# Loading and splitting the down weights at other stages in the last block of a hybrid decoder step

## The chip, the cores and the metric

The kernel runs on one core of one Trainium2 chip. The metric is device time in microseconds (us) of one execution, as a median over runs; it is compared with the kernel before on the same chip.

## The reference, cut to what matters

One decoder layer is computed in float32 for 2048 prompt positions and 32 sample rows (8 sequences of 4): attention and a gating unit, an output projection, and then a SwiGLU feed-forward network with 1024 model columns and 2816 hidden columns.

```python
def _swiglu(x, g, w_gate, w_up, w_down):
    h = _rmsnorm(x, g)
    return (jax.nn.silu(h @ w_gate) * (h @ w_up)) @ w_down
...
    x = x + jnp.concatenate([att, u * gate], axis=-1) @ w_out
    x = x + _swiglu(x, norm2_g, w_gate, w_up, w_down)
```

Only the last line, and in it the product with `w_down`, is concerned here, and that only for the last third of the positions.

## The kernel before

**Blocks and units.** The layer's second half runs over three blocks of tiles of 128 positions: six, six and four. The last block (`B.last`) holds four tiles and the 32 sample rows, whose two halves make five row groups for the down product. In each block the feed-forward network runs over 22 units `f`, one for each 128 hidden columns. A unit has seven stages `q` = 0 to 6, one for each of the seven products of a fast 2x2 matrix multiplication (`product`, L1596). Every float32 operand is held as a high part in a rounded format and a low part (the rest), and a product is made of three matmuls (high x high L1606, high x low L1607, low x high L1608) for each of four slices: 12 matmuls a stage, in the last block with 272 columns each.

**Operands of the products.** Stage `q` of unit `f` also prepares stage `q` of unit `f + 1` (`prepare`, L1570). In the last block ScalarE (ACT) makes the high part (`high`, L1543, its copy stands at L1545), GpSimd (POOL) makes the low part one stage later (`low_half`, L1547, its subtraction at L1549), and SyncE (SP) issues the load of the same source for unit `f + 2` (`load_source`, L1502, its DMA at L1504). Sources `fr` have eight buffers, so that load waits until POOL has made the low part of the source one stage before. Operand pairs `op` have eight buffers too; a high part is written into the buffer of a product that has just ended. In stages 1 and 3 SP also issues a piece of 512 KB of the sample cache's copy, from DRAM to DRAM (`roll`, L1255, DMA at L1258).

**Down weights.** The rows of `w_down` for unit `f`, 128 x 1024, are loaded by SP into `fd` (`load_down`, L1586, DMA at L1588), of which there is one buffer. `split_down` (L1592) splits it by `split_sb` (L132): ACT copies the high part (L135), POOL subtracts for the low part (L138), into a pair `dw`, of which there are two, one for even and one for odd units. `fd` is free for the next load when both have read it. The load of unit `f` is called behind stage 2 of unit `f` (that of unit 0 earlier), its split behind stage 6 where `f` is even, behind stage 5 where it is odd.

**Down product.** The down products of units `f - 2` and `f - 1` run together in the even unit `f`, row groups 0 and 1 behind stage 3, 2 and 3 behind stage 4, the sample rows behind stage 5 (`down_unit`, L1664, matmuls at L1679). A row group of 128 rows has two halves of six matmuls of 512 columns, three on the even unit's `dw` and then three on the odd unit's. The left operands `hw` are written by ACT (L1656, L1660) and DVE (L1274) when a unit ends. DVE adds the sums to the accumulator (L1681). For the last pair of units `last_rows` (L1728) does it, with its first matmuls in `first_downs` (L1683).

**What sets the order.** Each engine, SP's queue too, works through its instructions in the order in which the code calls them; a call that is put at another stage moves every instruction in it on each of these queues. Waits are semaphores that follow from the use of the buffers.

Of the kernel before, what the change touches and what calls it, by code (L numbers as in the profile page):

```python
# [28 lines left out]
NF = FF // P  # L29
# [35 lines left out]
def hymba_step(ctx: ExitStack, tc: tile.TileContext, A: dict, O: dict):  # L65
# [66 lines left out]
    def split_sb(hi, lo, src, eng_hi=None, eng_lo=None):  # L132

        if eng_hi is None:
            act.activation(hi, src, AF.Copy)  # L135
        else:
            eng_hi.tensor_copy(hi, src)
        (eng_lo or pool).tensor_sub(lo, src, hi.bitcast(F32))  # L138
# [540 lines left out]
    for half in range(2):  # L679
        for ki, kind in enumerate(ORDER[half]):  # L680
            for gi, tiles in enumerate(GROUPS):
# [13 lines left out]
                for j, tj in enumerate(tiles):  # L695
# [25 lines left out]
                    else:  # L721
                        layer_norm(e + 1, t, lambda t=t: zn["g", t], P, lambda t=t: gate_tile(t))

                        f = e + 4 + ((3 if half else 5) if tj in (4, 5) else 0)
# [510 lines left out]
    def op_tile():  # L1235

        t_ = pool_["fg"].tile([P, 2, 512], F32R, name="op", tag="op", bufs=8)
        return t_[:, 0], t_[:, 1]
# [6 lines left out]
    def ob_pair(name):  # L1245
        t_ = lo.tile([P, 2, 1024], F32R, name=name, tag="ob", bufs=2)
        return t_[:, 0], t_[:, 1]
# [7 lines left out]
    def roll(n):  # L1255
        for src, dst, b, q in pieces[:n]:
            r0, r1 = q * 256, min((q + 1) * 256, WB - ST)
            sync.dma_start(O[dst][b, r0:r1, :], A[src][b, ST + r0:ST + r1, :])  # L1258
        del pieces[:n]
# [10 lines left out]
    def tick():  # L1270
        clock[0] += 1
        while due and min(due)[0] <= clock[0]:
            fn, args = due.pop(min(due))
            fn(*args)  # L1274
# [35 lines left out]
    def load_wo(half, s, staged):  # L1310
        raws["o", half, s] = w_ = staged()
        r0 = (s + 4) % KD * P
        sync.dma_start(w_, A["w_out"][r0:r0 + P, half * 512:(half + 1) * 512])

    def split_wo(B, half, s, place, eng_lo=None):
        B.wo[half, s] = wh, wl = place(s)
        split_sb(wh, wl, raws.pop(("o", half, s)), eng_lo=eng_lo)
# [252 lines left out]
    def prepare(B, f, s):  # L1570

        if B.b0 == 0:
            for fn, j in (ODD_STAGES if f % 2 else EVEN_STAGES if f else FIRST_STAGES)[s]:
                fn(f, j)
            return
        for fn, j in ((low_half, s - 1), (high, s)):
            if 0 <= j < 7:
                fn(f, j)
        if s < 7 and f + 1 < NF:
            load_source(f + 1, s)  # L1580

    def ahead_of(f, s):
        for fn, j in (ODD_AHEAD if f % 2 else EVEN_AHEAD).get(s, ()):
            fn(f, j)

    def load_down(f):  # L1586
        raws["d", f] = w_ = pool_["fd"]
        sync.dma_start(w_, A["w_down"][f * P:(f + 1) * P, :])  # L1588
# [3 lines left out]
    def split_down(f):  # L1592
        wd[f % FC] = ob_pair("dw")
        split_sb(*wd[f % FC], raws.pop(("d", f)))
# [105 lines left out]
    def final_a(B, i, then=None):  # L1700
        n = B.rows[i]
        y = square_tile()
        if n == SR:
            act.activation(y[0:SR], B.acc[i][SR:2 * SR], AF.Copy)
            dve.tensor_add(B.acc[i][0:SR], B.acc[i][0:SR], y[0:SR])
        s1 = fl.tile([P, 4], F32, name="s1", tag="s1", bufs=6)
        act.activation(y[:n], B.acc[i][:n], AF.Square, accum_out=s1[:n, 0:1])
        later(1, rms_b, s1, n)
        later(2, final_b, B, i, s1, then)
# [92 lines left out]
    B = blocks[0]  # L1802
# [75 lines left out]
    def sources(B, f, *js):  # L1878
        for j in js:
            if B.b0 == 0:  # L1880
                load_quarter(f, j)
            else:
                load_source(f, j)
# [26 lines left out]
    def first_block(B):  # L1910

        m2, m1 = acc_place(2), acc_place(4)
        split_early(B, 1, m1)
        split_early(B, 2, m2)
        B.place()
        load_cat(B, 0, KD - 1, KD)
        load_cat(B, 5, 0, KD)
        merge_load(h, 2)
        load_acc(B, 1)
        load_acc(B, 0)  # L1920
        half1_load(*range(KD))
        sync.dma_start(gain[0], dap(A["final_g"], 0, [[0, P], [1, D]]))
        plan.run(10 ** 9)
        split_early(B, 3)
        for n, what in ((2, [(merge, h, 2, pool), (merge, h, 3, pool), (split_cat, B, 0), (split_early, B, 4)]),
                        (4, [(merge_store, h, 2, 4)]), (5, [(open_end, B, 1)]),
                        (6, [(half1_split, B, 0, 1)]), (7, [(open_end, B, 0), (split_cat, B, 5)]),
                        (8, [(half1_split, B, 2, 3)]), (9, [(half1_split, B, 4, 5), (sources, B, 0, 0, 1, 2, 3)]),
                        (10, [(half1_split, B, 6, 7)]), (11, [(sources, B, 1, 0, 1, 2, 3)])):
            later(n, both, *what)  # L1930
        for i in (1, 2, 3):
            open_unit(B, i)
        open_part(B, 0, (KD - 1,), False, True)
        for i in (4, 5):
            open_unit(B, i)
        first_operands(B)

        p2 = second_unit(B, 2)
        for i in (2, 3):
            load_acc(B, i)  # L1940
        second_end(B, 0, second_unit(B, 0))
        open_end(B, 2)
        second_end(B, 2, p2, 3)
        p1 = second_unit(B, 1)
        for i in (4, 5):
            load_acc(B, i)
        second_end(B, 1, p1)
        p3 = second_unit(B, 3)
        open_end(B, 3)
        second_end(B, 3, p3)  # L1950
        for i in (4, 5):
            open_end(B, i)
        for i in (4, 5):
            second_end(B, i, second_unit(B, i), 1)
# [54 lines left out]
    for bi, B in enumerate(blocks):  # L2009
        if bi == 0:  # L2010
            first_block(B)
        else:
            next_block(B, downs, finals)
        if B.last:
            hs4 = consts.tile([P, 4, 2 * SR], F32R, name="hs4", tag="cats")
        nb = None if B.last else blocks[bi + 1]

        part = 4
        units = [dict(f=f, a=0, b=B.nt) for f in range(NF)]
        if not B.last:  # L2020
            units[0:1] = [dict(f=0, a=0, b=part), dict(f=0, a=part, b=B.nt)]
        rows = list(range(len(B.rows)))
        last_h = {}

        def one(u, q):
            tick()
            product(B, u, q)
            f = u["f"]
            if u["b"] < B.nt:
                if bi == 0 and q in (0, 2):  # L2030
                    sources(B, 2, q, q + 1)
                return

            if f and q < 2:
                prepare(B, f, 7 + q)
            if f + 1 < NF:
                prepare(B, f + 1, q)
            if f + 2 < NF:
                if bi == 0 and f:
                    if q in (0, 2):  # L2040
                        sources(B, f + 2, q, q + 1)
                if bi == 0:
                    ahead_of(f + 2, q)
            elif nb:

                for s in {(0, 2): (0, 1), (0, 4): (2, 3), (1, 3): (4, 5), (1, 5): (6, 7)}.get((f + 2 - NF, q), ()):
                    load_wo(0, s, fraw)
                if f + 1 == NF and q > 0:
                    split_wo(nb, 0, q - 1, lambda s: op_tile())
            if f + 1 < NF and q in (1, 3, 5)[:(1, 3, 2)[bi]]:  # L2050
                roll(1)

            if q == 2 and f:
                load_down(f)
            elif q == (5 if f % 2 else 6):
                split_down(f)

        def downs_of(pair, a, b):
            for i in rows[a:b]:
                down_unit(B, i, pair)  # L2060

        for n, u in enumerate(units):
            u["n"] = n
            for q in range(7):
                one(u, q)
                if u["f"] % 2 == 0 and u["f"] > 0 and 3 <= q < 6:
                    downs_of((B.h[0], B.h[1]), *((0, 2), (2, 4), (4, 9))[q - 3])
        pair = (B.h[0], B.h[1])
        if B.last:
            last_rows(B, pair)  # L2070
        else:

            last = ([4] if nb.last else []) + [i for i in rows if not (nb.last and i == 4)]
            downs = [lambda B=B, pair=pair: first_downs(B, last[0], last[1], pair)]
            downs += [lambda B=B, pair=pair, i=i: down_unit(B, i, pair) for i in last[2:]]
            finals = [lambda B=B, nb=nb, i=i: final_a(B, i, (load_acc, nb, i) if i < len(nb.rows) else None) for i in last]
# [104 lines left out]
```

## Time and profile before

| | us |
|---|---|
| median of 3 runs | 2521.73 |
| lowest and highest | 2508.28 and 2523.93 |
| the profiled execution, its own time | 2527.26 |
| its span | 2525.4 |
| TensorE (PE) busy, share of the span | 97% |
| DVE, ACT, POOL busy | 50%, 45%, 52% |

The profile comes from one execution. In its rows, a group shows line, engine, operation, output and inputs, the number of instructions, busy time and mean duration, and then the idle time just ahead of them with the engine and line that ended it ("<-"). PE is the stream of matmuls, PEld that of weight loads. The last block's 22 units lie between about 2110 and 2500 us.

### The profile page before, as it was taken

Reading aid. Unit: us, or ns where it says so; the run is one execution under the profiler, and the core shown is the slowest. Engines: PE = TensorE matmul, PEld = TensorE weight load, DVE = VectorE, ACT = ScalarE, POOL = GpSimd, SP = SyncE. Lnnn points to the kernel's source line nnn. Section 1 sums busy time; section 2 is a strip of 40 time slices with the busy share of each in tenths; the row PEclk is TensorE's granted clock in tenths of the full one; section 3 lists DMA queues with packets and bytes.
Section 4 is the critical chain, followed back from the end, with each engine's and each line's share of the span. In section 5 each row is a group of like instructions: output and inputs, shape, how many; then the busy total and the mean of one; then the engine's idle time right before and its main releaser. Section 6 shows DMA issues by size and latency. Waiting matters only on the chain.

```text
span 2525.4 us, 39104 instructions
## 1 busy us (share of the span) xinstructions
PE 2442.6 (97%) x14022; PEld 2116.0 (84%) x14022; DVE 1270.2 (50%) x2595; ACT 1130.9 (45%) x2449; POOL 1303.2 (52%) x1019
## 2 busy tenths in 40 slices
PE   8998999999999899999999999999999998999997
PEld 7877776668887678999999989999999978888986
DVE  4558582217776645444444465444444465444444
ACT  7324343226666556454554446233233255333334
POOL 2216441005778447676776626445355445556565
PEclk9999999999999899999999999999999999999999
DMA  9974845675554554555555363535445363555553
GB/s 294 280 230 148 259 127 175 200 253 175 182 168 131 142 191 154 167 175 179 155 194 166 128 218 134 188 136 199 170 169 203 117 223 126 175 200 178 197 174 132
DMA packets 292292, 455.36 MB, mean 180 GB/s; under 512 B 28711, under 2 KB 160984, under 8 KB 286980
## 3 DMA queue, kind: packets, MB, share of 16 engines
q1 hardware_dynamic: 285252, 440.82, 53.6%
q10 hardware_dynamic: 6848, 12.06, 1.7%
q8 instruction: 111, 1.82, 0.3%
q14 instruction: 81, 0.66, 0.1%
HBM read 365.07 MB, written 157.84 MB: 207 GB/s over the span
## 4 chain that ended last, share of the span: by engine, by line
PE 62%; POOL 6%; issue 6%; DVE 3%; DMA 3%; ACT 2%; SPq 0%; POOLq 0%; DVEq 0%; ACTq 0%
PE ps_o L1679 15%; PE ps_m L1608 9%; PE ps_m L1607 9%; PE ps_m L1606 9%; POOL op L1549 4%; PE ps_s L856 3%; PE ps_o L911 2%; PE ps_t L883 1%; PE ps_s L935 1%; PE ps_s L318 1%; PE ps_o L1373 1%; PE ps_o L1375 1%; PE ps_o L1374 1%; PE ps_m L1373 1%; PE ps_m L1375 1%
## 5 line engine op out<-in xcount | busy, mean ns | idle before, releaser
L1549 POOL TENSOR_TENSOR op<-fr,op 128x512 fp32r<-128x512 f32 x385 | 487.5, 1299 | 246.6 <-ACT op L1545 232.5
L1606 PE MATMUL ps_m<-xh,op 128*128 128x384 f32 (+3 forms) x1904 | 604.9, 318 | 0.7 <-DVE zn L1627 0.4
L1608 PE MATMUL ps_m<-xh,op 128*128 128x384 f32 (+3 forms) x1904 | 604.4, 317 | 0.0
L1607 PE MATMUL ps_m<-xl,op 128*128 128x384 f32 (+3 forms) x1904 | 603.9, 317 | 0.1
L1679 PE MATMUL ps_o<-dw,hw 128*128 128x512 f32 x2040 | 492.6, 396 | 20.4 <-POOL dw L138 12.6
L1679 PEld LDWEIGHTS ps_o<-dw,hw 128*128 128x128 f32 x2040 | 385.1, 190 | 106.3 <-POOL dw L138 16.5
L1606 PEld LDWEIGHTS ps_m<-xh,op 128*128 128x128 f32 x1904 | 360.2, 189 | 5.3 <-ACT xh L1450 0.7
L1607 PEld LDWEIGHTS ps_m<-xl,op 128*128 128x128 f32 x1904 | 360.0, 189 | 4.0 <-DVE xl L1462 0.4
L1681 DVE TENSOR_TENSOR acc<-acc,ps_o 128x512 f32<-128x512 f32 (+1 forms) x362 | 248.3, 687 | 226.8 <-PE ps_o L1679 226.8
L1608 PEld LDWEIGHTS ps_m<-xh,op 128*128 128x128 f32 x1904 | 359.9, 189 | 0.0
L1646 ACT ACTIVATE ps_t<-zn 128x384 f32<-128x384 f32 (+1 forms) x126 | 58.5, 465 | 500.7 <-DVE zn L1629 423.8
L138 POOL TENSOR_TENSOR dw<-fd,dw 128x1024 fp32r<-128x1024 f32 x66 | 158.5, 2401 | 204.2 <-ACT dw L135 194.0
L1545 ACT ACTIVATE op<-fr 128x512 fp32r<-128x512 f32 x396 | 233.8, 626 | 3.4 <-PE ps_m L1375 3.4
L318 PE MATMUL ps_s<-wh,xh 128*128 128x512 f32 x480 | 196.8, 410 | 6.0 <-ACT xh L135 6.0
L320 PE MATMUL ps_s<-wh,xl 128*128 128x512 f32 x480 | 189.0, 394 | 0.0
L319 PE MATMUL ps_s<-wl,xh 128*128 128x512 f32 x480 | 188.9, 394 | 0.0
L1549 POOL TENSOR_TENSOR op<-pair,op 128x512 fp32r<-128x512 f32 x63 | 81.3, 1298 | 113.7 <-ACT op L1545 109.3
L536 POOL TENSOR_TENSOR pr<-kv,qb 96x512 f32<-96x512 f32 x32 | 45.6, 1425 | 170.3 <-DMA kv<-in_cache_k_dram 86.1
L318 PEld LDWEIGHTS ps_s<-wh,xh 128*128 128x128 f32 x480 | 90.9, 189 | 48.5 <-issue 23.7
L1656 ACT ACTIVATE hw<-ps_t 128x384 fp32r<-128x384 f32 (+1 forms) x126 | 54.2, 449 | 157.7 <-DVE ps_t L1652 157.7
L927 POOL CAST sq<-k 128x512 fp32r<-128x512 f32 x32 | 34.1, 1066 | 164.8 <-PE ps_s L319 164.8
L1274 DVE TENSOR_TENSOR hw<-ps_t,hw 128x384 fp32r<-128x384 f32 (+1 forms) x120 | 59.3, 508 | 109.7 <-ACT hs L1660 57.0
(490 smaller groups left out, 4328.7 us busy)
## 6 DMA issues: line engine op xcount, KB each, us to landing
fr<-ab_d SPq DMA_DIRECT2D x308, 256.0 KB
fd<-in_w_down_dram SPq DMA_DIRECT2D x66, 512.0 KB
out_ks_dram<-in_cache_k_dram SPq DMA_DIRECT2D x56, 512.0 KB
out_vs_dram<-in_cache_v_dram SPq DMA_DIRECT2D x56, 512.0 KB
ab_d<-fr SPq DMA_DIRECT2D x88, 256.0 KB
qk_d<-pair SPq DMA_DIRECT2D x64, 256.0 KB
ab_d<-pair SPq DMA_DIRECT2D x63, 256.0 KB
kv<-in_cache_k_dram SPq DMA_DIRECT2D x64, 192.0 KB
```

The lines of the kernel that those rows point to most:

```text
L138: (eng_lo or pool).tensor_sub(lo, src, hi.bitcast(F32))
L318: pe.matmul(o[j], xh[:, k, :], wh, start=(k == 0), stop=False)
L319: pe.matmul(o[j], xh[:, k, :], wl, start=False, stop=False)
L320: pe.matmul(o[j], xl[:, k, :], wh, start=False, stop=(k == KD - 1))
L856: pe.matmul(s[:, a:b_], d[q][:, qs], d["k"][:, t0:t0 + b_ - a], start=(z == 0), stop=(z == 1))
L1545: act.activation(ops[f, j][0], ab[f][j], AF.Copy)
L1549: (pool if f or j in POOL_LOW else dve).tensor_sub(lo_, ab[f][j], hi.bitcast(F32))
L1606: pe.matmul(out, wh[:, ks], xh[:, :, k], start=(k == 0), stop=False)
L1607: pe.matmul(out, wh[:, ks], xl[:, :, k], start=False, stop=False)
L1608: pe.matmul(out, wl[:, ks], xh[:, :, k], start=False, stop=(k == 3))
L1679: pe.matmul(ps[0:nr], l_, r_[:, cs], start=(z == 0 and y == 0), stop=(z == FC - 1 and y == len(pairs) - 1))
L1681: dve.tensor_add(B.acc[i][0:nr, cs], B.acc[i][0:nr, cs], ps[0:nr])
```

## The change

In the last block alone, the load of a unit's down weights is called directly behind the split of the unit before, and the odd units' split moves from behind stage 5 to behind stage 3. The even units' split stays behind stage 6. The first two blocks keep the old places, and so does the load of unit 0. No instruction is added or taken out, and no tile or buffer count is changed.

```diff
-            if q == 2 and f:
+            if B.last:
+                if q == (3 if f % 2 else 6):
+                    split_down(f)
+                    if f + 1 < NF:
+                        load_down(f + 1)
+            elif q == 2 and f:
                 load_down(f)
             elif q == (5 if f % 2 else 6):
                 split_down(f)
```

On SP, in the middle of the last block (`fr` are sources of products, `fd` down weights, `out_vs_dram` the copied cache), before:

```order
L1504 DMA fr<-ab_d 128x512 x5
L1258 DMA out_vs_dram<-in_cache_v_dram 16x8192
L1504 DMA fr<-ab_d 128x512
L1588 DMA fd<-in_w_down_dram 128x1024
L1504 DMA fr<-ab_d 128x512
```

and now, over one odd unit and the even one behind it:

```order
L1588 DMA fd<-in_w_down_dram 128x1024
L1504 DMA fr<-ab_d 128x512 x5
L1258 DMA out_vs_dram<-in_cache_v_dram 16x8192
L1504 DMA fr<-ab_d 128x512 x2
L1258 DMA out_vs_dram<-in_cache_v_dram 16x8192
L1504 DMA fr<-ab_d 128x512 x3
L1588 DMA fd<-in_w_down_dram 128x1024
```

Before, `fd` stands in each unit between the two pieces of the cache, one source behind the first. Now it stands behind the seventh source of the even unit and, in the odd unit, directly behind a piece of the cache, and it waits there for POOL's part of the split.

On ACT, at the last odd unit with a unit behind it (L135 is the split's copy, L1545 the high parts, L1646 the two silu's of a unit, L1656 and L1660 the hidden values), before:

```order
L1616 ACTIVATE zn<-ps_m_24389 128x272
L1545 ACTIVATE op<-fr 128x512 x2
L1646 ACTIVATE ps_t_24444<-zn 128x272
L1545 ACTIVATE op<-fr 128x512 x3
L1646 ACTIVATE ps_t_24508<-zn 128x272
L1545 ACTIVATE op<-fr 128x512
L135 ACTIVATE dw<-fd 128x1024
L1656 ACTIVATE hw<-ps_t_24508 128x4x64
L1660 ACTIVATE hs_20687<-ps_t_24508 128x16
```

and now:

```order
L1616 ACTIVATE zn<-ps_m_24390 128x272
L1545 ACTIVATE op<-fr 128x512 x2
L1646 ACTIVATE ps_t_24445<-zn 128x272
L1545 ACTIVATE op<-fr 128x512 x2
L135 ACTIVATE dw<-fd 128x1024
L1545 ACTIVATE op<-fr 128x512
L1646 ACTIVATE ps_t_24512<-zn 128x272
L1545 ACTIVATE op<-fr 128x512
L1656 ACTIVATE hw<-ps_t_24512 128x4x64
L1660 ACTIVATE hs_20687<-ps_t_24512 128x16
```

The copy of the odd unit's down weights moves ahead of the fifth and sixth high part and of the unit's second silu.

On POOL, where the last block's units begin (L138 with `dw` is the split's subtraction, L1549 the low parts of the product's operands), before:

```order
L1549 TENSOR_TENSOR op<-fr,op 128x512 x6
L138 TENSOR_TENSOR dw<-fd,dw 128x1024
L1549 TENSOR_TENSOR op<-fr,op 128x512 x6
L138 TENSOR_TENSOR dw<-fd,dw 128x1024
L1549 TENSOR_TENSOR op<-fr,op 128x512 x8
L138 TENSOR_TENSOR dw<-fd,dw 128x1024
```

and now:

```order
L1549 TENSOR_TENSOR op<-fr,op 128x512 x6
L138 TENSOR_TENSOR dw<-fd,dw 128x1024
L1549 TENSOR_TENSOR op<-fr,op 128x512 x4
L138 TENSOR_TENSOR dw<-fd,dw 128x1024
L1549 TENSOR_TENSOR op<-fr,op 128x512 x10
L138 TENSOR_TENSOR dw<-fd,dw 128x1024
```

Between an even unit's split and the odd unit's there stand four low parts in place of six, and the two that are left out follow behind the split.

## The prediction

> **What bounds the kernel now.** I read first the page's costliest groups, then the waits of the last block, then that block cut into stretches, then one stretch in order of time. The page has PE busy for nearly the whole span, so only an idle PE can be won back. Its groups name one line of the last block that PE idles at, the down product:
>
> ```profile
> L1679 PE MATMUL ps_o<-dw,hw 128*128 128x512 f32 x2040 | 492.6, 396 | 20.4 <-POOL dw L138 12.6
> ```
>
> Of the 20.4 us, POOL's subtraction for the down weights ended 12.6. The waits between 2125 and 2492 us, the last block's units, tell who is behind that:
>
> ```profile
> POOL dw L138 <- ACT dw L135: 63.4, 17, 5.0
> ACT dw L135 <- DMA fd<-in_w_down_dram: 52.7, 10, 6.2
> PE ps_o L1679 <- POOL dw L138: 11.6, 10, 1.3
> PE ps_o L1679 <- ACT hw L1656: 4.5, 6, 1.2
> ```
>
> Read from below: PE waits ten times for POOL, six times for hidden values from ACT. POOL waits for ACT, and ACT waits ten times for the down weights' transfer, some 5 us each. There are ten pairs of an odd and an even unit here: in each the odd unit's load is late.
>
> The stretches run from one even unit's split on POOL to the next (columns: start and end, length, busy time and count of each engine, PE's granted clock, DMA share, GB/s):
>
> ```profile
> 2125.07:2164.04 38.97, 36.51 (x220) 32.51 (x219) 16.44 (x36) 13.21 (x31) 22.26 (x17) 0.91 0.52 176
> 2164.04:2201.96 37.92, 36.08 (x226) 32.36 (x225) 16.44 (x36) 13.20 (x31) 22.28 (x16) 0.95 0.55 180
> 2201.96:2237.22 35.26, 34.23 (x226) 31.24 (x225) 16.45 (x36) 13.21 (x31) 22.31 (x17) 1.00 0.56 194
> 2237.22:2273.73 36.51, 34.48 (x226) 31.22 (x225) 16.44 (x36) 13.20 (x31) 22.30 (x16) 1.00 0.55 188
> 2273.73:2311.39 37.66, 36.11 (x227) 32.40 (x225) 16.45 (x36) 13.21 (x31) 22.29 (x17) 0.95 0.53 182
> 2311.39:2349.86 38.47, 35.99 (x227) 32.33 (x225) 16.44 (x36) 13.20 (x31) 22.25 (x17) 0.96 0.53 178
> 2349.86:2384.57 34.71, 34.20 (x226) 31.23 (x225) 16.45 (x36) 13.21 (x31) 22.34 (x16) 1.00 0.58 197
> 2384.57:2419.57 35.00, 34.22 (x226) 31.23 (x225) 16.44 (x36) 13.21 (x31) 22.32 (x16) 1.00 0.56 196
> 2419.57:2455.46 35.89, 34.48 (x226) 31.23 (x225) 16.44 (x36) 13.21 (x31) 22.32 (x16) 1.00 0.55 191
> 2455.46:2492.07 36.61, 34.50 (x226) 31.23 (x225) 16.45 (x36) 13.21 (x31) 22.30 (x16) 1.00 0.40 137
> ```
>
> Equal work takes 34.71 to 38.97 us, 367.00 in all. Four stretches also lost clock.
>
> **What a pair costs when nothing waits.** The stretch from 2237 us, on PE, and the sample rows of a later one:
>
> ```profile
> 2250.70 0.86 PE L1679 MATMUL ps_o<-dw,hw 128*128 128x512 f32 x3
> 2252.27 0.50 PE L1679 MATMUL ps_o<-dw,hw 128*128 128x512 f32 x1 [0.70 <-ACT hw L1656]
> 2254.09 4.83 PE L1679 MATMUL ps_o<-dw,hw 128*128 128x512 f32 x20 [1.33 <-POOL dw L138]
> 2258.76 0.29 PE L1606 MATMUL ps_m<-xh,op 128*128 128x272 f32 x1
> 2260.28 5.63 PE L1679 MATMUL ps_o<-dw,hw 128*128 128x512 f32 x24
> 2265.75 0.29 PE L1606 MATMUL ps_m<-xh,op 128*128 128x272 f32 x1
> ```
> ```profile
> 2485.59 1.98 PE L1679 MATMUL ps_o<-dw,hs 128*64 128x512 f32 x8
> 2487.41 0.29 PE L1606 MATMUL ps_m<-xh,op 128*128 128x272 f32 x1
> ```
>
> A product takes 2260.28 - 2258.76 = 1.52 us, 24 down matmuls without a wait 2265.75 - 2260.28 = 5.47, the sample rows 2487.41 - 2485.59 = 1.82. A pair of units needs 14 x 1.52 + 2 x 5.47 + 1.82 = 34.04 us, ten need 340.4. **367.0 - 340.4 = 26.6 us are lost**, 2.66 a pair. The first 24 down matmuls show it: from 2250.70 to 2258.76 are 8.06 us for 5.47, a loss of 2.59, more than the 0.70 + 1.33 that the rows call idle.
>
> Part of the 26.6 is clock: each stretch's length times what its clock lacks is 38.97 x 0.09 + 37.92 x 0.05 + 37.66 x 0.05 + 38.47 x 0.04 = 8.8 us. The other 17.8 are waits.
>
> **The change, part by part.** SP, ACT and POOL in the same stretch:
>
> ```profile
> 2242.52 0.53 SPq L1258 DMA_DIRECT2D out_vs_dram<-in_cache_v_dram  x1
> 2243.76 0.43 SPq L1588 DMA_DIRECT2D fd<-in_w_down_dram  x1
> ```
> ```profile
> 2239.62 1.66 ACT L1545 ACTIVATE op<-fr 128x512 fp32r<-128x512 f32 x3
> 2243.81 0.40 ACT L1646 ACTIVATE ps_t<-zn 128x272 f32<-128x272 f32 x1 [2.53 <-DVE zn L1629]
> 2250.54 1.06 ACT L135 ACTIVATE dw<-fd 128x1024 fp32r<-128x1024 f32 x1 [5.77 <-DMA fd<-in_w_down_dram]
> ```
> ```profile
> 2237.22 2.40 POOL L138 TENSOR_TENSOR dw<-fd,dw 128x1024 fp32r<-128x1024 f32 x1 [3.48 <-ACT dw L135]
> 2239.57 7.52 POOL L1549 TENSOR_TENSOR op<-fr,op 128x512 fp32r<-128x512 f32 x6
> 2251.67 2.37 POOL L138 TENSOR_TENSOR dw<-fd,dw 128x1024 fp32r<-128x1024 f32 x1 [4.58 <-ACT dw L135]
> ```
>
> 1. *The odd unit's load moves up.* Now it is issued at 2243.76, behind a 512 KB piece of the cache, and ACT can start 6.78 us later. Yet its buffer is free from 2239.62, when POOL ends the even unit's split. Moved there it is issued at about 2239.7, 4.1 us earlier, with no piece of the cache ahead of it.
>
> 2. *How long the load then takes* (X, from issue to ACT's start). The trace has one such load, that of the last unit, which waited for POOL's split as all will now; and the longest of the others:
>
> ```profile
> 2494.50 0.34 SPq L1588 DMA_DIRECT2D fd<-in_w_down_dram  x1
> ...
> 2317.92 0.43 SPq L1588 DMA_DIRECT2D fd<-in_w_down_dram  x1
> ```
> ```profile
> 2499.00 1.04 ACT L135 ACTIVATE dw<-fd 128x1024 fp32r<-128x1024 f32 x1
> ...
> 2325.16 1.06 ACT L135 ACTIVATE dw<-fd 128x1024 fp32r<-128x1024 f32 x1 [6.23 <-DMA fd<-in_w_down_dram]
> ```
>
> The first has no idle ahead of ACT's copy: it had landed within 4.50 us. The other took 7.24 behind a piece of the cache. So X lies at 4.5 or under up to 7.24; I take 4.5, since the new issue has the first row's surroundings: an idle queue ahead.
>
> 3. *The odd unit's split moves up.* ACT reaches it after the second of the three high parts at 2239.62, at about 2240.7, and waits until 2239.7 + 4.5 = 2244.2; its copy ends at 2245.3. POOL has four low parts ahead (4 x 1.25 from 2239.57, until 2244.6), so its split runs from 2245.3 to 2247.7. The down matmuls that want it start at 2250.70: **the wait that now ends there is gone, with 3 us to spare.**
>
> 4. *What stands behind the new wait.* On POOL: the low part of product 3 of the even unit, which stood ahead of the split and now follows it, done at 2247.7 + 1.25 = 2248.95. PE starts that product one product ahead of the down matmuls, at 2250.70 - 1.52 = 2249.18, and wants the low part at its third matmul, 2249.4. Spare: 0.45 us. In general it is late by X - 4.95: the stall's next place, if X is longer. On ACT: the second silu, now at 2243.81, starts at about 2245.9, and the hidden values are ready some 2.5 us later (an estimate: six instructions of about 0.4 us, like the silu's row); PE wants those of the odd unit behind three matmuls of 5.47 / 24 = 0.23 us, at 2251.4. On SP: the load of the next `fr`, whose buffer POOL frees only behind the split, so it is not held further; from the fourth on these loads come some 2 to 3 us later, for high parts a unit later. All of this is covered; without the cover it is the 2 to 3 us, once a pair.
>
> 5. *The even unit's load* is issued behind the odd unit's split, about 2247.7, and POOL's part of its split starts at 2273.73, where the next stretch begins. 26 us cover a load of at most 7; without them it would be the odd unit's wait over again.
>
> 6. *The tail.* The last odd split waited for nothing; its copy may come up to a microsecond earlier or the last silu that much later. I count 0, between -1 and +1.
>
> **The sum.** The profiled execution took 2527.26 us; without the 26.6 it takes 2500.7. It lies 5.5 us above the median of the three runs, 2521.73. If the median run lost as many microseconds less in these waits, it too goes to 2500.7; if the 5.5 lie elsewhere, to 2495.1. I take the middle, **2498**, 23.7 us or 0.9% less. A measurement of this kernel tells about 1% from no change.
>
> **The rivals.** *The stall moves to product 3.* If the load's neighbours, four sources and a piece of the cache close behind it, stretch X to the middle between 4.95 and the 6.78 above, 5.9 us, PE waits 1.0 a pair for POOL's low part. 10 us stay, and half of the lost clock with them: 26.6 - 10 - 4.4 = 12 won, **2510**. For it: ACT idled 52.7 / 10 = 5.3 us on average for the odd units' loads, and it came to them after their issue, so they took longer still. Against: all those had a piece of the cache ahead.
>
> *The clock drops stay.* Behind one of the waits the clock halves:
>
> ```profile
> 2288.00:2291.00 3.00, 1.45 (x6) 0.93 (x6) 2.23 (x8) 2.99 (x8) 3.00 (x2) 1.00 0.15 51
> 2291.00:2294.00 3.00, 3.00 (x9) 2.35 (x8) 1.27 (x2) 1.16 (x3) 3.00 (x4) 0.50 0.39 102
> ```
>
> I take it that the 3 us with PE half idle cause the 3 us at 0.50. But the stretches from 2237 and 2455 us have waits as long and lost no clock. If the drops have another cause, only the waits are won, 17.8: **2504**. [...]
>
> *Slower.* The same place, product 3 behind POOL's split: when X passes 4.95 + 2.66 = 7.6 us, PE waits longer for the low part than it now waits for the down weights. At X = 8.6 that is 1 us a pair more, **2532**. The transfer would have to take more than the longest in the trace, 7.24, with less ahead of it.
>
> *The change does not reach it.* If the waits at L1679 were hidden values first of all (4.5 us of the list are), the time stays at **2520**. But ACT's L1656 stands behind its wait for the down weights in every such row.
>
> **How the numbers follow.** Forecast 0.62 (own range 2490 to 2505), moved stall 0.16, drops stay 0.12, slower 0.05, not reached 0.05. Faster by over 1% means under 2496.5: half of the forecast's chance, since that bound lies 1.5 us under its middle, and a little of the other cases, as other runs may have lost more than the profiled one: 0.36. Slower by over 1% needs 2.5 us more a pair, X at 10 us, 0.03; the rest, 0.61, is within 1%. The range reaches from 2488, under the forecast's own end, to 2514, which takes in the moved stall.
>
> **What would show it.** Right: PE's idle time at L1679 for POOL's L138 is gone; the pairs last about 34.0 us, ten close to 340; the clock reads 1.00 through them; ACT's wait for `fd` is still there, 3 to 4 us a pair, but ahead of the silu. The moved stall would show as PE waiting at L1608's weights or L1607 for POOL's L1549 in the even units. Wrong: pairs of 36 us or more with these waits gone; or a clock below 1 without a wait ahead of it.

## The result and the profile after

| | before | after |
|---|---|---|
| median of five runs, us | 2521.73 | 2496.71 |
| lowest and highest | 2508.28 and 2524.78 | 2495.61 and 2498.84 |
| the profiled execution | 2527.26 | 2497.53 |

The ratio is 0.990, with a 95% interval of 0.987 to 0.9931: 25.0 us less by the medians, 1.3 us under the forecast of 2498. The runs also lie closer together, 3.2 us from lowest to highest where it was 16.5. The last block, which alone is changed, holds four tiles, 512 of the 2048 positions: a quarter of them, not the third that is said above.

The line of the page that idled, now:

```profile
L1679 PE MATMUL ps_o<-dw,hw 128*128 128x512 f32 x2040 | 480.4, 391 | 4.1 <-DVE acc L1681 3.3
```

The idle time ahead of the down product fell from 20.4 to 4.1 us, and POOL's L138 is no longer what ends most of it. The waits of the ten pairs:

```profile
POOL dw L138 <- ACT dw L135: 38.3, 12, 3.5
ACT dw L135 <- DMA fd<-in_w_down_dram: 26.1, 10, 3.7
ACT op L1545 <- DMA fr<-ab_d: 14.0, 7, 2.9
```

ACT still waits ten times for the down weights, half as long as before, and seven times for a source, which is new. No row of PE is left among these waits. The stretches from one even unit's split to the next, the first three, the last, and their sum:

```profile
2123.96:2157.13 33.17, 33.17 (x220) 30.53 (x219) 16.42 (x36) 13.40 (x31) 22.33 (x17) 1.00 0.60 207
2157.13:2191.07 33.94, 33.94 (x226) 31.30 (x225) 16.41 (x36) 13.39 (x31) 22.30 (x16) 1.00 0.58 202
2191.07:2225.02 33.95, 33.95 (x226) 31.32 (x225) 16.42 (x36) 13.39 (x31) 22.33 (x16) 1.00 0.59 202
...
2428.70:2462.65 33.95, 33.95 (x227) 31.31 (x225) 16.42 (x36) 13.40 (x31) 22.31 (x17) 1.00 0.41 148
sum 338.69, PE 338.69 PEld 312.30 DVE 164.22 ACT 133.94 POOL 223.08; mean PE 33.87 PEld 31.23 DVE 16.42 ACT 13.39 POOL 22.31
```

Nine of the ten take 33.94 or 33.95 us, PE is busy for the whole of each, and the clock reads 1.00: the block now runs at the pace of its matmuls. Ten pairs went from 367.00 to 338.69 us, 28.3 less of the 29.7 that lie between the two profiled executions.

One pair in order of time, on SP, ACT, POOL and PE:

```profile
2227.45 0.33 SPq L1588 DMA_DIRECT2D fd<-in_w_down_dram  x1
```
```profile
2230.92 1.06 ACT L135 ACTIVATE dw<-fd 128x1024 fp32r<-128x1024 f32 x1 [2.35 <-DMA fd<-in_w_down_dram]
2231.89 0.61 ACT L1545 ACTIVATE op<-fr 128x512 fp32r<-128x512 f32 x1
2232.40 0.38 ACT L1646 ACTIVATE ps_t<-zn 128x272 f32<-128x272 f32 x1
```
```profile
2225.02 2.40 POOL L138 TENSOR_TENSOR dw<-fd,dw 128x1024 fp32r<-128x1024 f32 x1 [3.49 <-ACT dw L135]
2227.37 5.04 POOL L1549 TENSOR_TENSOR op<-fr,op 128x512 fp32r<-128x512 f32 x4
2232.35 2.42 POOL L138 TENSOR_TENSOR dw<-fd,dw 128x1024 fp32r<-128x1024 f32 x1
2234.71 11.33 POOL L1549 TENSOR_TENSOR op<-fr,op 128x512 fp32r<-128x512 f32 x9
```
```profile
2238.51 5.65 PE L1679 MATMUL ps_o<-dw,hw 128*128 128x512 f32 x24
```

POOL ends the even split at 2225.02 + 2.40 = 2227.42, SP issues the load at 2227.45, ACT starts 3.47 us later. POOL does four low parts meanwhile and takes the odd split at 2232.35 without a wait. The split is done at 2234.77 and its next low part at about 2236.0; the down matmuls start at 2238.51 and run through.

### The profile page after: what moved, and what is told of

Read it like the earlier page. It is cut to its first block, busy times and chain, and to the rows that moved or that the text cites. A ratio compares the mean times of both kernels' runs of the same rounds, so it can differ in the third digit from the quotient of the medians.

```text
span 2495.7 us, 39113 instructions
## 1 busy us (share of the span) xinstructions
PE 2433.8 (98%) x14022; PEld 2114.7 (85%) x14022; DVE 1268.0 (51%) x2595; ACT 1132.3 (45%) x2449; POOL 1303.2 (52%) x1019
## 4 chain that ended last, share of the span: by engine, by line
PE 73%; DVE 3%; POOL 2%; ACT 2%; issue 1%; DMA 1%; SPq 0%; DVEq 0%; ACTq 0%; POOLq 0%
PE ps_o L1679 19%; PE ps_m L1608 11%; PE ps_m L1606 11%; PE ps_m L1607 11%; PE ps_s L856 2%; PE ps_o L911 2%; PE ps_t L883 1%; PE ps_o L1373 1%; PE ps_s L935 1%; PE ps_o L1374 1%; PE ps_o L1375 1%; PE ps_s L318 1%; PE ps_s L320 1%; PE ps_m L1373 1%; PE ps_s L319 1%
## 5 line engine op out<-in xcount | busy, mean ns | idle before, releaser
L1549 POOL TENSOR_TENSOR op<-fr,op 128x512 fp32r<-128x512 f32 x385 | 487.8, 1302 | 257.6 <-ACT op L1545 243.5
L1606 PE MATMUL ps_m<-xh,op 128*128 128x384 f32 (+3 forms) x1904 | 605.0, 318 | 0.9 <-ACT xh L1450 0.5
L1608 PE MATMUL ps_m<-xh,op 128*128 128x384 f32 (+3 forms) x1904 | 604.5, 317 | 0.0
L1679 PE MATMUL ps_o<-dw,hw 128*128 128x512 f32 x2040 | 480.4, 391 | 4.1 <-DVE acc L1681 3.3
L1679 PEld LDWEIGHTS ps_o<-dw,hw 128*128 128x128 f32 x2040 | 380.4, 188 | 82.6 <-DVE acc L1681 5.1
L1606 PEld LDWEIGHTS ps_m<-xh,op 128*128 128x128 f32 x1904 | 360.3, 189 | 5.3 <-ACT xh L1450 0.7
L1608 PEld LDWEIGHTS ps_m<-xh,op 128*128 128x128 f32 x1904 | 360.0, 189 | 0.0
L1646 ACT ACTIVATE ps_t<-zn 128x384 f32<-128x384 f32 (+1 forms) x126 | 58.3, 463 | 474.1 <-DVE zn L1629 384.6
L1545 ACT ACTIVATE op<-fr 128x512 fp32r<-128x512 f32 x396 | 235.3, 624 | 23.5 <-DMA fr<-ab_d 14.0
L138 POOL TENSOR_TENSOR dw<-fd,dw 128x1024 fp32r<-128x1024 f32 x66 | 158.8, 2406 | 162.6 <-ACT dw L135 160.5
L1549 POOL TENSOR_TENSOR op<-pair,op 128x512 fp32r<-128x512 f32 x63 | 81.3, 1298 | 115.1 <-ACT op L1545 110.7
L1656 ACT ACTIVATE hw<-ps_t 128x384 fp32r<-128x384 f32 (+1 forms) x126 | 54.8, 451 | 162.1 <-DVE ps_t L1652 162.1
L320 PEld LDWEIGHTS ps_s<-wh,xl 128*128 128x128 f32 x480 | 91.5, 191 | 20.5 <-DVE xl L138 0.3
```

Of the source, the lines that this page charges most:

```text
L320: pe.matmul(o[j], xl[:, k, :], wh, start=False, stop=(k == KD - 1))
L1545: act.activation(ops[f, j][0], ab[f][j], AF.Copy)
L1549: (pool if f or j in POOL_LOW else dve).tensor_sub(lo_, ab[f][j], hi.bitcast(F32))
L1606: pe.matmul(out, wh[:, ks], xh[:, :, k], start=(k == 0), stop=False)
L1608: pe.matmul(out, wl[:, ks], xh[:, :, k], start=False, stop=(k == 3))
L1646: act.activation(g, c, AF.Silu)
```

## Experiments

Theory A is the prediction's: the odd unit's load is issued late, that is the whole loss, and what limits an earlier split is POOL's low part of product 3 behind it. Its rivals stand with each run. "Before" and "the change" name the two kernels; every ratio is to the kernel before on the same chip.

**The load alone.** The odd split goes back to stage 5.

```diff
-                if q == (3 if f % 2 else 6):
+                if q == (5 if f % 2 else 6):
```

> Last block: load directly behind the split of the former unit, odd split left behind stage 5. Theory A (the late issue of the odd unit's load is the whole loss): the load is in ACT's reach long before stage 5, POOL's split ends some 1.2 us before the down matmuls, pairs last 33.95 us as after the change, median 2497 (2494 to 2501). Rival B (the odd split's earlier stage is needed as well): POOL comes to the split only behind two more low parts and PE still waits for it, about 1 us a pair, median 2507 or more.

Measured: 2499.9 us, ratio 0.9897 (0.9874 to 0.992). The ten pairs in one row:

```profile
2123.54:2462.23 338.69, 338.69 (x2236) 312.28 (x2235) 165.21 (x360) 132.19 (x301) 222.81 (x160) 1.00 0.58 197
```

338.69 us, the same as with the change. The move of the load does it all; the earlier odd split adds nothing.

**The split alone.** The kernel before, with the odd split of the last block behind stage 3.

```diff
-            elif q == (5 if f % 2 else 6):
+            elif q == ((3 if B.last else 5) if f % 2 else 6):
```

> Last block: load behind stage 2 of its own unit as before, odd split behind stage 3. Theory A: ACT waits for the load at stage 3 until the same time as before, and POOL's low part of the even unit's product 3 now stands behind that wait: some 5.9 us of PE wait a pair (load 6.8 us from issue, then 1.1 + 2.4 + 1.3, wanted 5.7 us after the issue), pairs near 40 us, clock drops in most of them, median 2570 (2550 to 2590). Rival B (an earlier split can only help, since PE waits for the down weights alone): 2522 or less.

Measured: 2570.0 us, ratio 1.0179 (1.0154 to 1.0203): slower, by what theory A gave. The ten pairs, their waits and one of the places on PE:

```profile
2125.45:2535.30 409.85, 364.74 (x2237) 331.43 (x2235) 164.14 (x360) 133.73 (x301) 222.03 (x161) 0.92 0.48 163
```
```profile
PE ps_m L1606 <- ACT hs L1660: 32.4, 10, 4.5
PE ps_m L1608 <- POOL op L1549: 12.7, 10, 1.5
ACT dw L135 <- DMA fd<-in_w_down_dram: 90.1, 10, 10.3
```
```profile
2265.77 0.56 PE L1606 MATMUL ps_m<-xh,op 128*128 128x272 f32 x1 [4.48 <-ACT hs L1660]
2267.71 0.60 PE L1608 MATMUL ps_m<-xh,op 128*128 128x272 f32 x1 [1.15 <-POOL op L1549]
```

ACT waits up to 10.3 us with nothing won, and PE stands ahead of product 3, not at the down product. The second row is the low part that was named. The first is a wait that theory A had not named: by the code, product 3 writes the bank of PSUM that DVE's L1635 reads for the odd unit's last product. L1635 stands on DVE behind the multiplication with the second silu, and the silu stands on ACT behind the wait for the weights.

```profile
2264.84 0.45 DVE L1652 TENSOR_TENSOR ps_t<-ps_t,raw 128x272 f32<-128x272 f32 x1 [9.14 <-ACT ps_t L1646]
2265.20 0.43 DVE L1635 TENSOR_TENSOR raw<-raw,ps_m 128x272 f32<-128x272 f32 x1
```

L1635 ends at 2265.63 and PE goes on at 2265.77; the wait's row names ACT's L1660, but that writes `hs`, and L1606 reads `xh` and `op`. Of the two, the low part comes last, in each of the ten pairs:

```profile
2264.08 2.35 POOL L138 TENSOR_TENSOR dw<-fd,dw 128x1024 fp32r<-128x1024 f32 x1 [7.56 <-ACT dw L135]
```

POOL's split ends at 2266.43, the low part behind it takes some 1.25 us, and PE starts its third matmul, which needs it, at 2267.71. Without the wait for the bank PE would have run two matmuls earlier and stood at the third until the same time. So it is theory A's path that sets the loss, and the wait that it left out is hidden in it.

**The load one stage later, at both places of the split.** The odd unit's load goes behind stage 0 of its unit.

```diff
             if B.last:
+                if q == 0 and f % 2:
+                    load_down(f)
                 if q == (3 if f % 2 else 6):
                     split_down(f)
-                    if f + 1 < NF:
+                    if f % 2 and f + 1 < NF:
                         load_down(f + 1)
```

> As the change, but the odd unit's load one stage later, behind stage 0 of its unit (the even unit's load stays directly behind the odd split). Theory A: issue 1.5 us later, with a source just ahead and one just behind it, so ACT can start 2 to 3 us later than after the change; the low part of product 3 is then 0.8 to 1.5 us late in each pair and PE waits there for POOL's L1549, not at the down product: pairs of 34.8 to 35.5 us, median 2505 to 2512. Rival (there is more room than the 1 to 1.3 us worked out, or the wait falls elsewhere): 2497.

Measured: 2502.64 us, ratio 0.9906 (0.9882 to 0.9929).

```profile
2125.19:2471.94 346.75, 341.39 (x2236) 312.89 (x2235) 164.13 (x360) 133.84 (x301) 223.00 (x160) 1.00 0.56 192
```
```profile
PE ps_m L1608 <- POOL op L1549: 5.2, 9, 1.3
```

34.7 us a pair, 8.1 us more in all than the change: the stall moves to the named place, in nine of ten pairs. The time lies just under theory A's range, and in most pairs the wait is shorter than the 0.8 to 1.5 us that it gave; seven of the ten loads took 3.6 to 3.8 us.

The second run has the same edit and `q == (5 if f % 2 else 6)` for the split.

> As the run with the load behind stage 0, but with the odd split behind stage 5. Theory A: two low parts go ahead of the split on POOL, so the late load costs nothing: ACT starts 4 to 5 us before the down matmuls and the split ends about 1 us before them; 34.0 us a pair, median 2497 (2494 to 2502). Rival (the split itself is then late): PE waits at the down product 0.5 to 1 us a pair, 2502 to 2507.

Measured: 2497.6 us, ratio 0.9888 (0.9867 to 0.9909).

```profile
2122.67:2461.37 338.70, 338.70 (x2237) 312.31 (x2235) 165.20 (x360) 132.76 (x301) 222.82 (x161) 1.00 0.57 197
```

With the split at stage 5 the later load costs nothing. So the earlier split of the change is no gain of its own: it takes away room that the load may need.

**Lateness or a transfer ahead.** The kernel before, with the pieces of the cache behind stages 3 and 5 in the last block.

```diff
-            if f + 1 < NF and q in (1, 3, 5)[:(1, 3, 2)[bi]]:
+            if f + 1 < NF and q in ((1,), (1, 3, 5), (3, 5))[bi]:
```

> The kernel before, with one thing else: in the last block the two pieces of the cache's copy go behind stages 3 and 5 of a unit in place of 1 and 3, so none stands directly ahead of the down weights' load. Theory A1 (the loss came half from the late issue and half from the piece ahead of it): the load is issued at the same place, but ACT can start 4 to 4.8 us later in place of 6.1 on average; the odd split then ends 0 to 0.6 us too late, pairs of 34 to 34.6 us, no clock drops, median 2499 to 2505. Theory A2 (the late issue is all of it, the piece ahead costs little): ACT starts 5.5 us or more after the issue, pairs of 35.3 us or more, median 2512 or more.

Measured: 2504.14 us, ratio 0.9933 (0.9911 to 0.9955), as A1 gave.

```profile
2131.06:2475.96 344.90, 340.87 (x2237) 311.53 (x2235) 164.40 (x360) 132.05 (x301) 223.10 (x161) 1.00 0.58 194
```
```profile
PE ps_o L1679 <- POOL dw L138: 4.0, 6, 1.2
ACT dw L135 <- DMA fd<-in_w_down_dram: 37.9, 10, 4.6
```

With the load's own call untouched, 22.1 of the 28.3 us are gone, and the clock reads 1.00 over the ten pairs. By issue and start in the timelines, the odd loads of the ten pairs take 4.1 to 5.7 us here, 4.7 on average, where before they take 4.95 to 7.24, 6.2 on average. So the 512 KB just ahead of the load was a large part of what made it late. An earlier issue with a piece still just ahead was not run: every run here that issues the odd load earlier also has no piece just ahead of it.

**The change in all blocks, and the change again.**

```diff
-            if B.last:
+            if True:
                 if q == (3 if f % 2 else 6):
```

> The change applied to all three blocks. Theory A: in the first two blocks PE waits for down weights less than 1 us in all, so there is nothing to win, and their units are long enough to hide the split at stage 3: as the change, 2497 (2494 to 2501). Rival: there POOL and ACT have more to do in a unit, the waiting split holds the low parts up as in the run that moved the split alone, and PE waits in those blocks: 2502 or more.

> The change itself, unaltered, beside the two others on one chip: 2497 (2494 to 2501) by every theory; clock at 1.00 through the ten pairs if the drops come from the waits, drops in two or more of them if they come by themselves.

Measured: the change again 2499.61 us, ratio 0.9916 (0.9889 to 0.9944); in all blocks 2512.96, ratio 0.9971 (0.9953 to 0.9989). Theory A failed here: the first block got longer. Its ten pairs with the change, and with the change in all blocks:

```profile
983.83:1436.01 452.18, 451.40 (x2371) 421.69 (x2371) 200.46 (x338) 228.34 (x563) 322.41 (x239) 1.00 0.53 170
```
```profile
991.02:1459.99 468.97, 457.76 (x2372) 421.61 (x2371) 197.17 (x338) 229.99 (x563) 322.09 (x239) 1.00 0.52 167
```

16.8 us more. The waits of the second kernel in these stretches, on SP and on ACT (L1517 applies a gain to gate and up columns, which the first block alone loads raw):

```profile
SPq L1588 <- POOL dw L138: 227.1, 20, 18.7
```
```profile
ACT fr L1517 <- DMA fr<-in_w_gate_dram: 45.1, 10, 5.9
```

The load waits on SP's queue for POOL's split, and there the loads of gate and up columns stand behind it. That wait is not all extra time on SP: its waits for POOL in these pairs add up to 266.0 us, and with the change to 259.5, at other instructions. What is new is that ACT waits for gate columns, and 10.7 us for up columns; with the change it does not wait for either. How this reaches PE, whose waits for DVE at L1679 and L1606 add up to 6.7 and 4.5 us between 930 and 1560 us, was not followed. Ten pairs of the second block take 456.41 us, and 456.44 with the change, so there the change does nothing. One more run parts the load's place from the earlier split.

```diff
-            if B.last:
-                if q == (3 if f % 2 else 6):
+            if B.last or bi == 0:
+                if q == ((3 if B.last else 5) if f % 2 else 6):
```

> The change, and in the first block the load alone directly behind the split, with the odd split left behind stage 5. It tells what made the change in all blocks 13 us slower than the change in the last one. Theory S (SP's queue: the load waits there for POOL's split, and the loads of gate and up columns and the stores behind it wait with it): the wait is there whatever the split's stage, the first block is 10 to 17 us longer, median 2507 to 2514. Theory P (the earlier odd split, which ACT and POOL reach before its load has landed): nothing of it is left, median 2494 to 2501.

Measured: 2530.25 us, ratio 1.0037 (1.0023 to 1.005), 16 to 23 us beyond what theory S gave, and far from theory P.

```profile
984.25:1468.18 483.93, 462.79 (x2371) 424.58 (x2371) 198.09 (x338) 231.91 (x563) 321.81 (x238) 0.99 0.49 162
```
```profile
SPq L1588 <- POOL dw L138: 295.0, 21, 18.6
PE ps_o L1679 <- POOL dw L138: 11.3, 10, 1.2
```

The first of these rows covers 980 to 1480 us, one wait more than the ten pairs, which have 276.4 us in 20. The wait on SP is there without the earlier split, and longer, so theory P falls; theory S has the direction, but its number missed. Why the first block loses 31.8 us here and 16.8 with the split at stage 3 was not separated: with the split at stage 5 one wait on SP is 276.4 / 20 = 13.8 us long, where it was 227.1 / 20 = 11.4, and PE comes to wait for the down weights themselves.

## Why the prediction came out right

*The loss of 26.6 us.* Right and a little small: 28.3 us were won in the ten pairs. The step worked with 34.04 us a pair; nine pairs take 33.95 and the first 33.17, which makes up the 1.7 us between the two. How much of the loss was clock and how much waits was not measured apart: both went together.

*The odd load's issue.* Right: it follows the end of POOL's split by 0.03 us.

*The load's time X.* Right in kind, 1 us long in size. I took 4.5 us, the upper bound of the one load that was like the new ones; nine of the ten take 3.43 to 3.60 us and one 4.82. The run with the pieces moved speaks for the nearest row: with no piece just ahead, X falls from 6.2 to 4.7 us on average at the same place of issue.

*The split and what stands behind it.* Right. The wait at the down product is gone; the low part of product 3 is ready about 1.3 us before its matmul, where the longer X had left 0.45. That this is the stall's next place is shown twice, at 8.1 us in the run with the load one stage later and at 71 us with the split alone. One wait was left out, that for the bank freed behind the second silu. With the change it costs nothing: in the pair shown, L1635 ends at 2233.61 and product 3 starts at 2236.99. With the split alone PE stands at it, but the low part comes later still.

*The even unit's load and the tail.* Right: ACT's ten waits for down weights are those of the odd units alone, and from the last pair to the end of the span it takes 33.0 us where it took 33.3.

*The sources' loads.* Right that it costs nothing, though it can be seen: ACT waits 14.0 us for sources, and PE does not.

*The median.* The result lies between the two bounds, but that it lies within 1.3 us of their middle is partly luck. The loss was 1.7 us larger than counted, the runs of before spread over 16.5 us, and the change run again has a median of 2499.61. The profiled executions differ by 29.7 us and the medians by 25.0; that would fit a median run that lost less in these waits, but no run at the median was profiled.

*The rivals.* The moved stall did not come, since X stayed under 4.95. The clock rival fell: with the waits gone the clock reads 1.00 through the ten pairs, in both profiles of the change and in those of the load alone, of the load behind stage 0 with the split at 5, and of the change in all blocks. A slower kernel by way of product 3 exists, at 2570.0 us, but it takes the split's move without the load's. That the change would not reach the wait is out.

## What to carry to other kernels

When an engine waits for a transfer, look at when its buffer came free and at what was issued just ahead of it on its queue: here taking away the 512 KB piece in front won 22.1 us of the ten pairs' 28.3 with the issue where it was, and an earlier issue with no piece in front won all of it. When a consumer is to be called earlier, look at when its data lands: here ACT's wait for the down weights, up to 10.3 us, then stood in front of the second silu, and the split moved alone cost 47 us. When a load is to wait on a queue for another engine, look at what is queued behind it: here that was free in the last two blocks and went with a loss of 17 to 32 us in the first, where ACT then waits for the gate and up columns behind it, 45.1 and 10.7 us with the change in all blocks.

## What the runs showed of the hardware

With the change, nine of ten odd loads of 512 KB take 3.43 to 3.60 us from issue to use, and one 4.82. With the pieces of the cache behind stages 3 and 5 they take 4.1 to 5.7 us, and behind a 512 KB copy from DRAM to DRAM and a source 4.95 to 7.24 us. What makes the middle case longer than the first was not tried.

The clock reads low behind some of PE's waits. With the split alone PE waits 4.48 us and then 1.15 in the pair shown above; the clock reads 0.80 in the wait and 0.59 in the 6.3 us behind it:

```profile
2261.50:2265.70 4.20, 0.00 (x0) 0.00 (x0) 0.83 (x3) 2.75 (x6) 1.62 (x1) 0.80 0.09 36
2265.70:2272.00 6.30, 5.08 (x19) 4.48 (x20) 2.63 (x8) 4.48 (x12) 6.30 (x6) 0.59 0.37 109
```

Over the ten pairs of that run it reads 0.92. The ten waits at L1606 add up to 32.4 us, 3.24 on average and 4.5 at most; those at L1608 to 12.7 us, 1.5 at most.

Before the change it read 0.91 to 0.96 in four of ten pairs, with waits of 1.35 us at most, two of them close together. Like waits did not always go with a drop: behind 0.20 and 1.35 us it read 0.50 from 2291 to 2294 us, and with 0.70 and 1.33 us, the second until 2254, it read 1.00 over the pair. In the run with the load behind stage 0 and the split at stage 3, with nine waits of up to 1.3 us at L1608, it reads 1.00 over the ten pairs. What decides between these was not tried.
